# A layer norm moved from ScalarE to VectorE inside a matmul-bound decoder layer, with its loads asked for one job sooner

## The chip, the cores and the metric

The kernel runs on one core of one Trainium2 chip. The metric is the device time of one execution in microseconds (us), and the median of several executions stands for a kernel. A profile of one more execution gives the start and duration of every instruction on each engine: TensorE (PE; its weight loads are listed as PEld), VectorE (DVE), ScalarE (ACT), GpSimd (POOL) and SyncE (SP), which here issues nearly all DMAs.

## The reference

One layer of a hybrid decoder is computed for 64 sample tokens and 1024 prompt tokens, in float32. Only the branch that the change touches is shown in full:

```python
h = rmsnorm(x, norm_mix)
q, k, v, gu, gv, ga, gb = split_in(h @ w_in)
o = sink_attention(q, k, v, mask, sinks)               # window 128, banded blocks
vn = layernorm(gelu(gv), ln_g, ln_b)                   # over 768 channels, one row per token
s = gelu(gu) * (tril(W_s[g]) @ vn + b[g])              # inside 128-token chunks, 6 groups
x = x + (sigmoid(ga) * (o @ w_pa) + sigmoid(gb) * (s @ w_pb)) @ w_out
x = x + conv_ffn(rmsnorm(x, norm_ffn))                 # up, causal conv of width 3, gelu gate, down
y = rmsnorm(x, norm_final)
```

`vn` of the sample tokens is also an output (`gvs`), beside keys, values and convolution states.

## The kernel before

Every large product is made of three passes of a rounded type: an operand is split into a high part (an ACT cast) and a low part (a DVE subtraction, line 41), and TensorE adds high times high, high times low and low times high. Nearly all of TensorE's time goes into such matmuls. Weights are streamed from HBM by SP, summed (line 178) and split on ACT and DVE a few units ahead of their use.

The tokens form two groups: group 0 has 576 columns (the 64 samples and four blocks of 128 prompt tokens), group 1 has 512 (four blocks). The work begins with the token-major projections `gv` and `v` (line 535). For these, `stats_tok` (line 495) sums the squares of each token on TensorE with one-column matmuls against ones, and ACT and DVE turn the sums into a scale that every evacuation of that stage uses. The result of `gelu(gv)` is written to HBM, one tensor `gvd` of 128 by 768 for each block of tokens.

Then come 19 pairs of output blocks by a seven-product scheme (class `Chain`, line 317): the loop over `seq` runs seven products j for each pair, twelve matmuls for each group in each product. A chain writes its products into a few PSUM banks again and again, and between two products on one bank ACT copies the intermediate sum out (`keep`, lines 296 and 298) or DVE adds it to a result (`put`, line 303). After the last product ACT writes one quarter (line 343), and `a_finish` applies gelu (line 852) or sigmoid (line 854) on ACT.

Side work is handed out between the products from lists of small jobs. After the ninth pair the list `lns` gives one job after each of the products 0, 2, 4 and 6: nine layer-norm jobs (`ln_job`), six entries that prepare the mixing and its samples, and twelve `mix_job`s that multiply the normalised blocks with the lower-triangular weights (lines 788 and 816, results in a PSUM tile called `mx`). What is left in the list is run at once when the last three pairs begin, and after it the list `prep` prepares the attention of the samples; there POOL copies the sample queries into a padded tile (line 892).

A layer-norm job loads one block `v` into one of two buffers, normalises it with one ACT instruction (line 759), multiplies by the gain and adds the bias on DVE (lines 761 and 762), and stores it to `vnd`, from which the mixing jobs read. The first job also opens the pool of these tiles, loads gain and bias, and computes mean, deviation and the factors `sd` and `mr` (lines 735 to 738); four of the jobs load half blocks of group 1 through the staging ring of four buffers and take their statistics (lines 754 and 755).

The program text does not fix the order on the engines alone. A planner sorts the instructions of each engine by their place in the text, its own cost estimates and the moment when buffers come free, so that an instruction that is ready can be issued ahead of earlier ones; a tile of a pool waits until an earlier tile in its buffer has been read for the last time. `keep_in_program_order` marks instructions that the planner may not move in this way.

The kernel ends with the down projection (line 1686) and the final norm. For the last 256 columns `fin_rms` sums squares by one-column matmuls (line 1719), ACT and DVE form the scale, and `fin_rb` spreads it over the partitions by matmuls with the identity (line 1731). Three matmuls of constants (line 1857) stand in the text between the two.

Of the kernel before, what the change touches and what calls it, by code (L numbers as in the profile page):

```python
# [6 lines left out]
F32 = mybir.dt.float32  # L7
F32R = mybir.dt.float32r
I32 = mybir.dt.int32
AF = mybir.ActivationFunctionType  # L10
ALU = mybir.AluOpType
# [4 lines left out]
P = 128  # L16
# [9 lines left out]
GW = 768  # L26
# [8 lines left out]
def layer(tc, a):  # L35
    nc = tc.nc
    V, S, G, PE = nc.vector, nc.scalar, nc.gpsimd, nc.tensor
# [11 lines left out]
    with ExitStack() as top:  # L49
# [18 lines left out]
        ones = cst.tile([P, P], F32, name="c_ones")  # L68
# [276 lines left out]
        def pick(x, place, lo, hi):  # L345
# [3 lines left out]
        groups = [dict(g=0, n=576, off=0, soff=NS, base=192, mbase=448, blk0=0,  # L349
                       chunks=[(192, 0, 320), (512, 320, 576)],  # L350
                       toks=[("s", 0), *((i, NS + P * i) for i in range(4))]),
                  dict(g=1, n=512, off=576, soff=0, base=0, mbase=0, blk0=4,
                       chunks=[(0, 0, 512)], toks=[(4 + i, P * i) for i in range(4)])]
# [15 lines left out]
        gvd = {name: dr(f"gvd{name}", [P, GW]) for gr in groups for name, _ in gr["toks"]}  # L369
# [13 lines left out]
        with ExitStack() as ph1:  # L383
# [9 lines left out]
            def stage(n):  # L393
                return stg.tile([P, 576], F32, name="stg")[:, :n]

            late = {}
# [90 lines left out]
            lnst = c1.tile([P, 9, 3, 6], F32, name="lnst")  # L487
            line(c1, 96)
            pso = ExitStack()
            psa = pso.enter_context(tc.tile_pool(name="psa", bufs=7, space=PSUM))  # L490

            def bank():
                return psa.tile([P, 512], F32, name="st")

            def stats_tok(g):

                acc = rsg[g]
                pt = bank()[:, :len(groups[g]["toks"])]
                for i, (_, lo) in enumerate(groups[g]["toks"]):
                    PE.matmul(pt[:, i:i + 1], acc[:, lo:lo + P], ones[:, 0:1], start=True, stop=True)  # L500
                S.activation(rstg[g], pt, AF.Sqrt, bias=eps, scale=1.0 / D)  # L501
                V.reciprocal(rstg[g], rstg[g])
# [120 lines left out]
            def first_out():  # L623
                stats_tok(0)
                for i in range(len(toks0)):
                    gv_out(0, i, 0, ps5[i])
# [58 lines left out]
            none = lambda: None  # L685
            jobs = [lambda: x_in(0)] + [x for kk in range(4) for x in (t0_job(kk), none)] + [t1_job(kk) for kk in range(4)]
            tokens(1, ("v", 1), lambda i, ps: v_out(1, i, ps), jobs, lambda: stats_tok(1))
            stats_all(1)
            wide["again"] = True
# [8 lines left out]
            def poola(name, bufs, stack=None, **kw):  # L698
                return (stack or pa).enter_context(tc.tile_pool(name=name, bufs=bufs, reuse_waits="tile", **kw))
# [27 lines left out]
            lno = ExitStack()  # L727

            def ln_scale(g):

                n = len(groups[g]["toks"])
                mv = late["lnp"].tile([P, 5, 2], F32, name="mv", bufs=2)[:, 0:n]
                sd, mr = (late[x][:, 5 * g:5 * g + n] for x in ("sd", "mr"))
                for t in range(n):
                    V.bn_aggr(mv[:, t], lnst[:, 5 * g + t, 0:3 - g])
                S.activation(sd, mv[:, :, 1], AF.Sqrt, bias=eps)
                V.reciprocal(sd, sd)
                V.scalar_tensor_tensor(mr, mv[:, :, 0], -1.0, sd, ALU.mult, ALU.mult)

            def ln_job(g, i):  # L740
                def go():
                    if "lnp" not in late:
                        lnp = late["lnp"] = poola("ln", 1, lno)
                        for x in ("lng", "lnb"):
                            late[x] = lnp.tile([P, GW], F32, name=x)
                            nc.sync.dma_start(late[x], a[x])
                        for x in ("sd", "mr"):
                            late[x] = lnp.tile([P, 9], F32, name=x)
                    if i == 0:
                        ln_scale(g)  # L750
                    if g == 0 and i < 4:
                        for e in range(2):
                            x = stage(384)
                            nc.sync.dma_start(x, gvd[groups[1]["toks"][i][0]][:, 384 * e:384 * e + 384])
                            V.bn_stats(lnst[:, 5 + i, e], x)
                    lnp, name = late["lnp"], groups[g]["toks"][i][0]
                    v = lnp.tile([P, GW], F32, name="v", bufs=2)
                    nc.sync.dma_start(v, gvd[name])
                    S.activation(v, v, AF.Identity, bias=late["mr"][:, 5 * g + i:5 * g + i + 1],
                                 scale=late["sd"][:, 5 * g + i:5 * g + i + 1])  # L760
                    V.tensor_mul(v, v, late["lng"])  # L761
                    V.tensor_add(v, v, late["lnb"])
                    nc.sync.dma_start(vnd[g][:, :, i], v.rearrange("p (g c) -> p g c", c=P))
                    if name == "s":
                        nc.sync.dma_start(a["gvs"], v[0:NS])
                return go

            lns = [ln_job(gr["g"], i) for gr in groups for i in range(len(gr["toks"]))]

            def mix_first():  # L770
                lno.close()
# [889 lines left out]
        with ExitStack() as ph3:  # L1661
# [64 lines left out]
            def fin_rb(ps, rt, nb, m):  # L1726

                both = [ps, psl.tile([P, 512], F32, name="fs", bufs=2)]
                for p in both:
                    for i in range(nb):  # L1730
                        PE.matmul(p[:, i * m:i * m + m], rt[:, i:i + 1].to_broadcast([m, P]), ident[0:m, 0:m],
                                  start=True, stop=True)
                return [p[:, :nb * m] for p in both]
# [20 lines left out]
            def fin_copy(th, e, rb):  # L1754
                rs = lp.tile([P, 288], F32, name="rb", bufs=2)[:, :spans[e][1] - spans[e][0]]
                copy = S.copy(rs, rb[-1])
                if not (th and e):
                    tc.keep_in_program_order(copy)
                return rb[0], rs
# [16 lines left out]
            bank = [psd.tile([P, 512], F32, name="dn") for _ in range(6)]  # L1776
# [77 lines left out]
                y_out(1, 0, c, c + 4)  # L1854
            fin[3] = fin_rms(1, 1, last)
            for _ in range(3):
                PE.matmul(bank[0][:, 0:P], ones, ones, start=True, stop=True)
            rb, rs = fin_copy(1, 1, fin_rb(*fin[3]))
            for c in range(0, KD, 2):
                fin_mul(1, 1, *((rb, (c,), V) if c < 6 else (rs, (c,), G)))  # L1860
# [94 lines left out]
```

## Time and profile before

| What | Value |
|---|---|
| median of 3 runs | 1507.31 us (1506.05 to 1512.88) |
| the profiled execution | 1507.61 us |
| its span on the core | 1505.9 us |
| mean granted TensorE clock | 0.998 |
| TensorE matmul busy | 1491.5 us (99%) |
| TensorE weight loads busy | 1451.8 us (96%) |
| VectorE busy | 1176.4 us (78%) |
| ScalarE busy | 856.3 us (57%) |
| GpSimd busy | 265.7 us (18%) |

The profile's times count from the start of the span; the profiled execution is 1.7 us longer than its span. A timeline row gives start, duration, engine, line and operation, the tile written and the tiles read, and how often it was repeated; in square brackets stands how long the engine had been idle before it, and what it waited for. Neighbouring instructions of one form are merged in a row. A row of windows gives for each engine its busy time and in brackets the instructions that started there, then the granted clock, the busy share of the DMA engines and what they moved in GB/s.

### The profile page before, as it was taken

How to read it: one execution, taken by the hardware profiler on the slowest of the kernel's cores; microseconds unless marked ns; L12 is line 12 of the kernel's file. 1: busy time of each engine (PE TensorE's matmuls, PEld its weight loads, DVE VectorE, ACT ScalarE, POOL GpSimd, SP SyncE). 2: the span in 40 equal slices, each digit the busy share in tenths (PEclk: the TensorE clock that was granted, in tenths of full speed). 3: DMA queues.
4: the chain of work that ended last, by engine and by line, in shares of the span. 5: the costliest groups of instructions: out<-in, count | busy, mean ns of one | idle time of the engine just before them, and what ended most of it. 6: DMA issues, size and time to landing. Idle time of an engine off the chain costs nothing.

```text
span 1505.9 us, 30082 instructions
## 1 busy us (share of the span) xinstructions
PE 1491.5 (99%) x11508; PEld 1451.8 (96%) x11508; DVE 1176.4 (78%) x1886; ACT 856.3 (57%) x1790; POOL 265.7 (18%) x375
## 2 busy tenths in 40 slices
PE   9999999999999999999999999999999999999998
PEld 9999999999998989998989999999999999999998
DVE  7798776755576887989667988898899888785586
ACT  7657676654465765864443555555555556363464
POOL 0001000110030222320134321332242222000002
PEclk9999999999999999999999999999999999999999
DMA  7688446864779757438988423232242226993453
GB/s 253 225 275 274 155 163 224 243 207 150 239 243 294 219 180 231 162 123 308 335 295 287 141 109 122 98 142 108 83 151 109 84 83 223 326 303 98 113 172 148
DMA packets 134431, 289.88 MB, mean 192 GB/s; under 512 B 15760, under 2 KB 36560, under 8 KB 134288
## 3 DMA queue, kind: packets, MB, share of 16 engines
q1 hardware_dynamic: 134144, 287.96, 56.8%
q8 instruction: 90, 1.47, 0.4%
q14 instruction: 53, 0.43, 0.1%
q10 hardware_dynamic: 144, 0.01, 0.0%
HBM read 198.97 MB, written 90.92 MB: 192 GB/s over the span
## 4 chain that ended last, share of the span: by engine, by line
PE 85%; DVE 5%; ACT 4%; DMA 3%; issue 2%; POOL 1%; SPq 0%; POOLq 0%; ACTq 0%; DVEq 0%
PE st L317 45%; PE dn L1686 14%; PE mm L242 13%; PE st L535 6%; PE po L1233 2%; PE sc L1182 1%; DVE wl L41 1%; PE pt L1209 1%; DMA v<-gvd 1%; PE mx L816 1%; ACT wh L41 1%; ACT s L1199 1%; DMA kd<-q 0%; DMA v<-gvds 0%; DVE v L761 0%
## 5 line engine op out<-in xcount | busy, mean ns | idle before, releaser
L317 PE MATMUL st<-t,wh 128*128 128x288 f32 x2128 | 428.6, 295 | 3.4 <-ACT k L296 2.3
L317 PEld LDWEIGHTS st<-t,wh 128*128 128x128 f32 x2128 | 335.7, 188 | 4.6 <-ACT k L296 3.0
L317 PE MATMUL st<-t,wl 128*128 128x288 f32 x1064 | 312.2, 293 | 0.0
L317 PE MATMUL st<-th,wh 128*128 128x256 f32 x1064 | 296.0, 278 | 0.6 <-ACT k L296 0.5
L317 PE MATMUL st<-tl,wh 128*128 128x256 f32 x1064 | 294.7, 277 | 0.0
L317 PE MATMUL st<-th,wl 128*128 128x256 f32 x1064 | 294.5, 277 | 0.0
L317 PEld LDWEIGHTS st<-th,wh 128*128 128x128 f32 x1064 | 200.0, 188 | 1.9 <-ACT k L296 1.4
L317 PEld LDWEIGHTS st<-t,wl 128*128 128x128 f32 x1064 | 200.1, 188 | 0.0
L317 PEld LDWEIGHTS st<-th,wl 128*128 128x128 f32 x1064 | 199.8, 188 | 0.0
L317 PEld LDWEIGHTS st<-tl,wh 128*128 128x128 f32 x1064 | 199.8, 188 | 0.0
L1686 PE MATMUL dn<-th,wh 128*128 128x288 f32 (+1 forms) x616 | 177.1, 288 | 0.6 <-ACT zb L343 0.6
L1686 PE MATMUL dn<-tl,wh 128*128 128x288 f32 (+1 forms) x616 | 176.8, 287 | 0.0
L41 ACT CAST wh<-wraw 128x512 fp32r<-128x512 f32 (+2 forms) x188 | 129.4, 701 | 82.0 <-DMA wraw<-wt 30.1
L1686 PE MATMUL dn<-th,wl 128*128 128x288 f32 (+1 forms) x616 | 175.3, 285 | 0.0
L41 DVE TENSOR_TENSOR wl<-wraw,wh 128x512 fp32r<-128x512 f32 (+2 forms) x188 | 148.0, 800 | 28.5 <-ACT wh L41 26.2
L41 ACT CAST wh<-ws 128x512 fp32r<-128x512 f32 x168 | 102.5, 621 | 93.9 <-PE st L317 53.0
L41 DVE TENSOR_TENSOR wl<-ws,wh 128x512 fp32r<-128x512 f32 x168 | 117.5, 710 | 44.5 <-ACT wh L41 43.7
L1686 PEld LDWEIGHTS dn<-th,wh 128*128 128x128 f32 x616 | 115.7, 188 | 1.0 <-ACT zb L343 0.8
L1686 PEld LDWEIGHTS dn<-th,wl 128*128 128x128 f32 x616 | 116.1, 188 | 0.1
L1686 PEld LDWEIGHTS dn<-tl,wh 128*128 128x128 f32 x616 | 115.7, 188 | 0.1
L535 PE MATMUL st<-w2h,hh 128*128 128x256 f32 x288 | 80.6, 280 | 0.4 <-ACT rst L501 0.4
L535 PE MATMUL st<-w2h,hl 128*128 128x256 f32 x288 | 80.1, 279 | 0.1
(281 smaller groups left out, 3169.1 us busy)
## 6 DMA issues: line engine op xcount, KB each, us to landing
wraw<-wt SPq DMA_DIRECT2D x137, 512.0 KB
traw<-td SPq DMA_DIRECT2D x77, 272.0 KB
td<-za SPq DMA_DIRECT2D x22, 544.0 KB
q<-qd SPq DMA_DIRECT2D x16, 512.0 KB
upd<-hl SPq DMA_DIRECT2D x14, 512.0 KB
td<-t SPq DMA_DIRECT2D x11, 544.0 KB
wpart<-wt SPq DMA_DIRECT2D x22, 256.0 KB
qd<-q SPq DMA_DIRECT2D x8, 576.0 KB
```

The costliest lines, as they stand in the source:

```text
L41: for x in (S.copy(hi, src), V.tensor_sub(lo, src, hi.bitcast(F32))):
L242: PE.matmul(ps[:, lo:lo + c1 - c0], u[:, k, :], v[:, c0:c1], start=(k == 0 and i == 0), stop=(k == nk - 1 and i == 2))
L317: PE.matmul(ps, u[:, kk, :], v, start=first and kk + i == 0, stop=kk == 3 and i == 2, skip_group_check=True)
L535: PE.matmul(ps, u[:, lo:lo + P], v[:, k, :], start=k + i == 0, stop=k == KD - 1 and i == 2)
L816: PE.matmul(ps[:, P * i:P * i + P], vn[:, i], late["wst"][:, c, :], start=True, stop=True)
L1182: PE.matmul(ps[:, h, o0:256], q, kst[kv][:, e, k0:cur + P], start=e == 0, stop=e == 1)
L1199: S.activation(s[:, h], s[:, h], AF.Exp, bias=nm[:, h:h + 1], accum_out=dn[:, h:h + 1])
L1209: PE.transpose(pt[:, h * P:h * P + P], s[:, h, 0:P], ident)
L1233: PE.matmul(po, v[:, kv, :], t, start=e == 0, stop=last)
L1686: PE.matmul(place(m, e), u[:, m, :], v[:, lo:hi], start=new and i + k == 0 and (e == 0 or m % 2 == 0), stop=i == NU - 1 and k == 2, skip_g ...
```

## The change

Three places are edited.

In `stats_tok` the small PSUM tile comes from the one-bank tag `mx` and no longer from the seven banks called `st`.

In the layer norm the ACT instruction is gone. Two DVE instructions with two operations each do the whole normalisation: (v + mr) * gain, then (result * sd) + bias; for this `mr` is now minus the mean and no longer minus the mean times the scale. The loads of a job are moved into a function `ln_load`, which the job before calls at its end. A new first entry of the list opens the pool and asks for the tiles of job 0, so the list is one entry longer, and every job in it comes one place later than before; each load of a block keeps the place that its job had.

At the end the three constant matmuls are marked to stay in program order.

```diff
             def stats_tok(g):
 
                 acc = rsg[g]
-                pt = bank()[:, :len(groups[g]["toks"])]
+                pt = psa.tile([P, 512], F32, name="mx", bufs=1)[:, :len(groups[g]["toks"])]
...
                 S.activation(sd, mv[:, :, 1], AF.Sqrt, bias=eps)
                 V.reciprocal(sd, sd)
-                V.scalar_tensor_tensor(mr, mv[:, :, 0], -1.0, sd, ALU.mult, ALU.mult)
-
-            def ln_job(g, i):
+                V.tensor_scalar(mr, mv[:, :, 0], -1.0, None, ALU.mult)
+
+            ln_toks = [(gr["g"], i, name) for gr in groups for i, (name, _) in enumerate(gr["toks"])]
+            ln_in = {}
+
+            def ln_load(at):
+
+                if at == 0:
+                    lnp = late["lnp"] = poola("ln", 1, lno)
+                    for x in ("lng", "lnb"):
+                        late[x] = lnp.tile([P, GW], F32, name=x)
+                        nc.sync.dma_start(late[x], a[x])
+                    for x in ("sd", "mr"):
+                        late[x] = lnp.tile([P, 9], F32, name=x)
+                if at < len(ln_toks):
+                    g, i, name = ln_toks[at]
+                    xs = [stage(384) for e in range(2)] if g == 0 and i < 4 else []
+                    for e, x in enumerate(xs):
+                        nc.sync.dma_start(x, gvd[groups[1]["toks"][i][0]][:, 384 * e:384 * e + 384])
+                    v = late["lnp"].tile([P, GW], F32, name="v", bufs=2)
+                    nc.sync.dma_start(v, gvd[name])
+                    ln_in[at] = xs, v
+
+            def ln_job(at):
                 def go():
...
+                    g, i, name = ln_toks[at]
+                    xs, v = ln_in.pop(at)
                     if i == 0:
                         ln_scale(g)
...
-                    S.activation(v, v, AF.Identity, bias=late["mr"][:, 5 * g + i:5 * g + i + 1],
-                                 scale=late["sd"][:, 5 * g + i:5 * g + i + 1])
-                    V.tensor_mul(v, v, late["lng"])
-                    V.tensor_add(v, v, late["lnb"])
+                    for e, x in enumerate(xs):
+                        V.bn_stats(lnst[:, 5 + i, e], x)
+                    col = slice(5 * g + i, 5 * g + i + 1)
+                    V.scalar_tensor_tensor(v, v, late["mr"][:, col], late["lng"], ALU.add, ALU.mult)
+                    V.scalar_tensor_tensor(v, v, late["sd"][:, col], late["lnb"], ALU.mult, ALU.add)
                     nc.sync.dma_start(vnd[g][:, :, i], v.rearrange("p (g c) -> p g c", c=P))
                     if name == "s":
                         nc.sync.dma_start(a["gvs"], v[0:NS])
+                    ln_load(at + 1)
                 return go
 
-            lns = [ln_job(gr["g"], i) for gr in groups for i in range(len(gr["toks"]))]
+            lns = [lambda: ln_load(0)] + [ln_job(at) for at in range(len(ln_toks))]
...
             fin[3] = fin_rms(1, 1, last)
             for _ in range(3):
-                PE.matmul(bank[0][:, 0:P], ones, ones, start=True, stop=True)
+                tc.keep_in_program_order(PE.matmul(bank[0][:, 0:P], ones, ones, start=True, stop=True))
```

More of the change, by code (lines that the diff above doesn't have):

```diff
@@ L737, in ln_scale @@
                 V.reciprocal(sd, sd)
-                V.scalar_tensor_tensor(mr, mv[:, :, 0], -1.0, sd, ALU.mult, ALU.mult)
-            def ln_job(g, i):
-                def go():
[L742 to L748, printed above, removed]
+                V.tensor_scalar(mr, mv[:, :, 0], -1.0, None, ALU.mult)
@@ L749, in go @@
+            def ln_job(at):
+                def go():
+                    g, i, name = ln_toks[at]
+                    xs, v = ln_in.pop(at)
                     if i == 0:
                         ln_scale(g)
[L751 to L759, printed above, removed]
-                                 scale=late["sd"][:, 5 * g + i:5 * g + i + 1])
-                    V.tensor_mul(v, v, late["lng"])
-                    V.tensor_add(v, v, late["lnb"])
+                    for e, x in enumerate(xs):
+                        V.bn_stats(lnst[:, 5 + i, e], x)
```

## The prediction

> **What bounds the kernel now.** I read the page's busy line first, then TensorE's own waits, then windows of 20 us to find where those waits lie, and last the timeline around each.
>
> ```profile
> span 1505.9 us, 30082 instructions
> PE 1491.5 (99%) x11508; PEld 1451.8 (96%) x11508; DVE 1176.4 (78%) x1886; ACT 856.3 (57%) x1790; POOL 265.7 (18%) x375
> ```
>
> TensorE is busy for 1491.5 of 1505.9 us. The change takes no matmul away, so all it can win lies in the missing 14.4 us and in matmuls that go slowly; what it can lose has no such limit. Less work on ACT, DVE or POOL counts only where TensorE waits for them. The profiled execution took 1507.61 us, 0.30 above the median of 1507.31, and 1.7 above its span; I sum against 1507.61 and take off 0.30 at the end.
>
> ```profile
> PE st L317 <- ACT k L296: 2.8, 4, 1.5
> PE st L317 <- ACT kn L298: 1.0, 1, 1.0
> ...
> 260.00:280.00 20.00, 20.00 (x166) 20.00 (x165) 12.70 (x18) 11.51 (x23) 2.57 (x2) 1.00 0.71 230
> 280.00:300.00 20.00, 19.14 (x153) 18.80 (x153) 15.41 (x21) 12.79 (x25) 2.73 (x2) 1.00 0.82 239
> 300.00:320.00 20.00, 17.50 (x141) 17.10 (x140) 13.49 (x19) 10.27 (x20) 2.31 (x2) 1.00 0.66 202
> ```
>
> TensorE's largest waits are for ACT's copies out of PSUM, and the windows put them into the layer norm: from 280 to 320 us TensorE is idle for 0.86 + 2.50 = 3.36 us. It starts 153 + 141 matmuls where the undisturbed window starts 166 each, 38 too few; at 20.00/166 = 0.120 us that is 4.6 us. So 3.4 (idle alone) to 4.6 (with slow matmuls after each stop) is what this stage can return.
>
> **The three stops.** The timeline shows each stop, and what stood ahead of the copy on ACT.
>
> ```profile
> 294.99 0.53 PE L317 MATMUL st<-t,wh 128*128 128x288 f32 x2 [0.86 <-ACT k L296]
> 308.19 0.53 PE L317 MATMUL st<-t,wh 128*128 128x288 f32 x2 [1.02 <-ACT kn L298]
> 318.78 0.54 PE L317 MATMUL st<-t,wh 128*128 128x288 f32 x2 [1.49 <-ACT k L296]
> ...
> 280.75 1.03 ACT L759 ACTIVATE v<-v,mr,sd 128x768 f32<-128x768 f32 x1 [3.54 <-DMA v<-gvd]
> 289.38 0.69 ACT L852 ACTIVATE z<-z 128x576 f32<-128x576 f32 x1 [3.11 <-DVE z L303]
> 291.75 1.02 ACT L759 ACTIVATE v<-v,mr,sd 128x768 f32<-128x768 f32 x1
> 294.55 0.39 ACT L296 COPY k<-st 128x288 f32<-128x288 f32 x1
> 303.69 1.03 ACT L759 ACTIVATE v<-v,mr,sd 128x768 f32<-128x768 f32 x1 [4.83 <-DMA v<-gvd]
> 305.77 1.03 ACT L759 ACTIVATE v<-v,mr,sd 128x768 f32<-128x768 f32 x1 [1.05 <-DVE v L761]
> 307.74 0.67 ACT L298 ACTIVATE kn<-st 128x288 f32<-128x288 f32 x2
> 315.85 1.03 ACT L759 ACTIVATE v<-v,mr,sd 128x768 f32<-128x768 f32 x1 [1.18 <-DMA v<-gvd]
> 318.35 0.38 ACT L296 COPY k<-st 128x288 f32<-128x288 f32 x1
> ...
> 281.81 0.96 DVE L761 TENSOR_TENSOR v<-v,lng 128x768 f32<-128x768 f32 x1 [3.06 <-ACT v L759]
> 288.91 0.44 DVE L303 TENSOR_TENSOR z<-k,st 128x288 f32<-128x288 f32 x1
> ```
>
> ACT runs in order. While its line-759 instruction waits for a load, the copies behind it wait too, and TensorE cannot write the bank again. With line 759 gone, even if no load lands sooner:
> - Second stop: ahead of the kn at 307.74 stood 4.83 us of waiting, two v of 1.03 and a wait of 1.05. Without the last three alone kn comes 3.1 us sooner, against 1.02 needed.
> - Third stop: 1.18 + 1.03 = 2.2 us sooner, against 1.49.
> - First stop: 1.02 us from the v at 291.75. ACT also waited 3.11 us for DVE's z of 288.91, which stood behind DVE's wait of 3.06; DVE starts at the landing, 280.75, rather than at 281.81, another 1.06. Together 2.1 against 0.86.
>
> **The layer norm, edit by edit.**
>
> ```profile
> L759 ACT ACTIVATE v<-v,mr,sd x9: 1020/1032/1035, 262.8 to 315.8; 128x768 f32<-128x768 f32 x9
> L761 DVE TENSOR_TENSOR v<-v,lng x9: 947/958/959, 263.9 to 316.9; 128x768 f32<-128x768 f32 x9
> L1426 DVE SCALAR_TENSOR_TENSOR x<-x,c_gains,sc 128x576 f32<-128x576 f32 x8 | 6.2, 804 | 0.0
> L1565 DVE SCALAR_TENSOR_TENSOR c<-za,cw,c 128x1104 f32<-128x1104 f32 x22 | 30.1, 1367 | 16.6 <-ACT c L1564 16.5
> ...
> SPq L758 <- DMA vnd<-v: 3.4, 3, 3.0
> ```
>
> ACT loses 9 x 1.03 = 9.3 us. DVE keeps 18 instructions. The new form is shown at 576 and 1104 elements (0.80 and 1.37 us); a straight line between them gives 1.01 us at 768, an estimate, against 0.958 for the old. That is 0 to 18 x 0.05 = 0.9 us more DVE work, hidden by DVE's idle time (15.41 and 13.49 busy of 20 in the two windows); without that cover it would cost the 0.9. `mr` stays two instructions on a handful of columns, with one input fewer, and counts nothing.
>
> The DMAs are the same in number and size. Each load keeps its place in the text and its job comes one place later, which gives the load a place more to land in. I count nothing for that: there are two buffers, and SP three times waited at a load for the store that frees one (3.4 us, up to 3.0). The half-block loads and their statistics have other buffers and nobody near. Behind each load on SP stand weight loads and stores; that queue is as long as before.
>
> So the stage returns 3.4 to 4.6 us by the static shift. DVE can now stop at a late load itself, with the weight splits and the puts behind it. I take 3.4, the idle time.
>
> **The list.** Eighteen entries behind the nine jobs move by one place, 48 matmuls or 5.8 us. They fill the seven pairs exactly (28 places), so no batch is left over. TensorE does the same matmuls elsewhere. What follows, the samples' preparation, I count as zero between a loss of 5.8 and nothing; no row excludes a gain but none suggests one.
>
> **The end.**
>
> ```profile
> 1496.33 0.71 ACT L1705 ACTIVATE sq<-x 128x256 f32<-128x256 f32 x2
> 1496.83 0.75 PEld L1857 LDWEIGHTS dn<-c_ones 128*128 128x128 f32 x6
> 1497.50 0.97 PEld L1719 LDWEIGHTS fs<-c_ones,sq 128*128 128x128 f32 x8
> 1498.60 0.26 ACT L1722 ACTIVATE rt<-fs,c_eps 128x2 f32<-128x2 f32 x1 [0.76 <-PE fs L1719]
> 1499.11 1.16 PE L1731 MATMUL fs<-c_ident,rt 128*128 128x128 f32 x8 [0.55 <-DVE rt L1723]
> ```
>
> The planner put the constant matmuls (six, as each is two passes) ahead of the last eight sums, from 1496.83 to 1497.50. The last squares end at 1497.04. In text order four sums can start at 1496.83 and four at about 1497.3, and all behind comes 0.67 us sooner. The constants then take 0.67 us of the 1497.50 to 1499.11 in which TensorE now works 0.97 us and waits 0.55; they end about when line 1731 becomes ready, which may give back 0.1. I take 0.6, between 0 (the mark does not move them) and 0.67. All that follows hangs on line 1731, so it reaches the end.
>
> **The statistics' bank.**
>
> ```profile
> 24.76 0.38 PE L535 MATMUL st<-w2h,hh 128*128 128x256 f32 x1 [0.36 <-ACT rst L501]
> 25.66 1.28 ACT L566 ACT_TABLE_LOAD   x1
> 26.95 1.21 ACT L566 ACTIVATE gv<-st,rst 128x256 f32<-128x256 f32 x3
> ```
>
> The 0.36 us goes, since the next tile finds a free bank. But that tile is 24 matmuls of about 0.12 us (the rate of the windows), 2.8 us, and the one after it needs a bank that the first of the three gv frees at 26.95 + 1.21/3 = 27.35. Today it begins at about 24.76 + 2.8 = 27.5; it cannot begin before 27.35. What is late next is this gelu, behind its table load of 1.28 us. Between 0 and 0.36, I take 0.1, near the gv row.
>
> **Sum.** 3.4 + 0.6 + 0.1 = 4.1; 1507.61 - 4.1 = 1503.5, on the median's scale 1503.2.
>
> **The rivals.**
> - Full return: 4.6 + 0.67 + 0.36 = 5.6, to 1501.7. For it: each stop's margin is 0.7 us or more. Against it: the planner orders anew.
> - The wait changes its engine: DVE stops at the loads, and half of the stage's gain stays away. 1507.31 - 1.7 - 0.6 = 1505.0. For it: ACT waited up to 4.83 us for a load, and DVE has more queued behind it. Against it: DVE stood through 3.06 us already, behind ACT. It holds if loads land no sooner, and with two buffers a load waits for the store two jobs before it. In the Trainium skill, "DMA: Bandwidth & Descriptors", section "Anatomy of one DMA — SWDGE (gpsimd) path", a transfer costs about 2.0 us fixed plus its bytes over 436 GB/s, an estimated 2.9 us for these 384 KB and 5.8 us for a store and the load behind it. By that rule a buffer is away for a whole place, asking sooner wins nothing, and DVE goes on waiting, so the result would be this rival's 1505.0. The trace, with ACT's waits of 3.54 and 4.83 us for loads, agrees so far; it is why the case has 0.2.
> - Slower, by the later places: the samples' queries are copied on POOL just ahead of the chains' POOL work.
>
> ```profile
> 428.36 6.97 POOL L892 COPY qs<-stg 64x64 f32<-64x64 f32 x16
> 435.73 0.91 POOL L327 TENSOR_TENSOR kn<-kn,ku 128x256 f32<-128x256 f32 x1 [0.40 <-ACT ku L296]
> ```
>
> Only 0.40 us lies between. If the copies move by the full place, 5.8 us, POOL's kn comes up to 5.4 us late, then z, the sigmoid on ACT that waits for z, and the next copies out of PSUM. It decides where more than 4.1 of these reach TensorE; the whole gives 1503.2 + 5.4 = 1508.6. Against it: the copies need only their load, and today start late because of their tile.
> - The mark moves nothing: 1503.8.
>
> **How the numbers follow.** My forecast (1502.4 to 1504.4, with the unmoved mark) has 0.45, the full return 0.17, DVE's wait 0.2, the slower rival 0.1; 0.08 is left for an order that the planner changes far from here, either way. The likeliest is 1503.2. The range 1501.0 to 1508.7 takes in all four cases. A measurement of this kernel can tell about 0.5%, 7.5 us, from no change: no case named reaches that. Faster by more needs 1499.8, beyond the full return, 0.05; slower by more needs 1514.8, 0.04; within, 0.91.
>
> **What would show it.** Right: no line-759 row, TensorE near 20.00 in both windows from 280 to 320 with about 166 matmuls each; line 1857 behind the last line 1719, and 1722 some 0.6 us nearer to the last line 1686; no wait for rst but one for gv within 0.5 us near 27. DVE's wait would read as DVE v waiting for the DMA, with TensorE waiting for wl or z there. The slower rival would show as line 327 behind the copies and idle TensorE from 435 to 450. Wrong I would be if new stops appear in stages that the text leaves alone.

## The result, and the profile after

The changed kernel takes 1514.9 us (median; 1509.6 to 1519.9) where the kernel before takes 1507.6 us: a ratio of 1.0045, 95% interval 1.0034 to 1.0056. It is slower, by less than 0.5% but outside the range predicted. The profiled execution took 1513.9 us.

Busy times of the kernel after, from the page:

```profile
span 1512.2 us, 30063 instructions
PE 1493.4 (99%) x11508; PEld 1453.4 (96%) x11508; DVE 1174.3 (78%) x1886; ACT 849.2 (56%) x1781; POOL 273.2 (18%) x375
```

ACT lost 7.1 us and DVE 2.1 us of work; POOL, which the change does not touch, is busy 7.5 us longer with the same 375 instructions. That row is the first hint. TensorE's waits in the kernel after (engine, line, released by: us in total, times, longest):

```profile
PE st L317 <- ACT k L296: 3.8, 4, 1.9
PE dn L1696 <- DVE x L1706: 2.9, 2, 2.0
PE pt L1133 <- DVE s L1126: 1.4, 1, 1.4
...
PE sc L1099 <- issue: 0.8, 1, 0.8
```

Waits for `x` of line 1706, `pt` of 1133 (1.4, before 0.4) and an unexplained pause at `sc` are new. To place them I took the start of the same TensorE matmul in both traces and subtracted. Columns are times in the trace of before; each row is one execution, up to 2.8 us away from the median of its kernel; the kernels below the first two rows come from the experiments.

```
TensorE later than before (us), at   28.1  285.5    346   452   490  1290  1312  1495
after                                -0.6   -0.9   -3.7  -1.5   0.7   1.5   6.4   6.2
after_again                           0.5    0.0   -3.5   0.7   1.4   1.3   5.0   5.2
four_more_on_act                     -0.3   -0.4   -3.0   1.1   1.1   1.0   1.0   0.9
state_on_act                         -0.1    0.7   -2.1   2.3   3.3   7.9   7.9   7.7
copies_late                          -0.3    1.9   -0.7   0.3   3.1   3.1   3.1   3.3
shift_alone                          -0.0    1.2    0.9   3.0   6.7   7.4   7.4   7.3
one_empty_less                        0.1    1.4   -1.7  -1.7  -1.3  -0.2  -0.2  -0.4
two_ops_alone                        -0.4    0.4   -0.9  -0.4  -0.2  -0.4  -0.4  -0.5
mark_alone                            0.1    0.7   -0.4  -0.1   0.6   0.7   0.7   0.6
bank_alone                            0.1    0.4    0.2   0.2   1.0   2.4   2.4   2.2
three_buffers                        -0.0   -0.6   -4.1  -4.1  -3.8  -3.5  -3.5  -3.6
three_old_bank                       -0.4   -0.4   -4.3  -4.2  -2.7  -2.5  -2.5  -1.9
```

Read the first row by differences: the layer norm won 2.8 us (285 to 346), then 4.4 us were lost between 346 and 490, and 4.9 us between 1290 and 1312. The other rows say how far such a difference can be trusted. With the old layer norm mark_alone still wins 1.1 us from 285 to 346, bank_alone loses 1.4 us once between 490 and 1290, and the two executions of after differ by 2.0 us from 346 to 452.

**The layer norm.** Windows of the kernel after (us, then busy time and count of PE, PEld, DVE, ACT, POOL, clock, DMA share, GB/s):

```profile
280.00:300.00 20.00, 20.00 (x164) 19.95 (x163) 15.04 (x23) 8.90 (x20) 3.85 (x2) 1.00 0.79 250
300.00:320.00 20.00, 18.84 (x154) 18.64 (x153) 15.54 (x24) 9.94 (x22) 1.50 (x2) 1.00 0.67 217
```

153 and 141 matmuls have become 164 and 154. Two of the three stops are gone; the third is left, and ahead of it DVE now waits for a load and does the layer norm, while ACT waits for DVE:

```profile
315.10 0.54 PE L317 MATMUL st<-t,wh 128*128 128x288 f32 x2 [1.16 <-ACT k L296]
...
305.23 1.02 DVE L770 SCALAR_TENSOR_TENSOR v<-v,mr,lng 128x768 f32<-128x768 f32 x1 [1.42 <-DMA v<-gvd]
...
310.44 0.69 ACT L862 ACTIVATE z<-z 128x576 f32<-128x576 f32 x1 [6.69 <-DVE z L303]
```

**After the mixing.** Timeline of the kernel after:

```profile
420.97 0.32 SPq L831 DMA_DIRECT2D sd<-stg  x1
...
425.52 0.58 SPq L897 DMA_DIRECT2D stg<-qsd  x1
...
428.94 8.16 POOL L902 COPY qs<-stg 64x64 f32<-64x64 f32 x16 [5.11 <-DMA stg<-qsd]
437.18 0.74 POOL L327 TENSOR_TENSOR kn<-kn,ku 128x256 f32<-128x256 f32 x1
437.99 1.06 POOL L303 TENSOR_TENSOR z<-kn,k 128x256 f32<-128x256 f32 x1
...
439.09 1.15 ACT L864 ACTIVATE z<-z 128x512 f32<-128x512 f32 x2 [2.77 <-POOL z L303]
440.71 0.36 ACT L296 COPY k<-st 128x256 f32<-128x256 f32 x1
...
441.12 0.39 PE L317 MATMUL st<-th,wh 128*128 128x256 f32 x1 [1.88 <-ACT k L296]
```

and the one row of before that the prediction did not show:

```profile
419.06 0.42 SPq L887 DMA_DIRECT2D stg<-qsd  x1
```

TensorE is 3.7 us ahead here, and yet the queries' load is issued 6.5 us later than before: the planner put it behind the store of the next to last mixing job (line 831) and the stores of z, because the mixing jobs now end one place later. POOL waits 5.11 us for it, kn comes 1.5 us later than before on the clock (435.73), 5.2 us against TensorE, then z, the sigmoid, the copy out of PSUM, TensorE.

What this stop costs depends on the clock. In after the clock stays at 1.00 behind it, and 2.2 us go from 346 to 452. In the second execution, after_again, the stop is 2.40 us long, the granted clock behind it is 0.50, and 4.2 us go:

```profile
443.00:445.00 2.00, 2.00 (x12) 2.00 (x11) 2.00 (x5) 1.51 (x4) 0.00 (x0) 0.50 0.90 287
```

**At 1300 us.** First the kernel before, ACT, POOL and SP:

```profile
1252.79 1.31 ACT L1564 ACTIVATE c<-za,cw 128x1104 f32<-128x1104 f32 x1 [2.15 <-DVE za L303]
...
1259.87 0.28 POOL L1577 COPY za<-stc 128x18 f32<-128x18 f32 x1 [4.31 <-DMA za<-zd]
1262.96 1.26 POOL L1562 COPY stc<-za 128x2 f32<-128x2 f32 x1 [0.98 <-DVE za L303]
...
1265.53 0.34 SPq L1812 DMA_DIRECT2D tails<-stc  x1
```

then the kernel after, in which every engine has the same order of instructions here:

```profile
1254.38 1.31 ACT L1574 ACTIVATE c<-za,cw 128x1104 f32<-128x1104 f32 x1 [2.43 <-DVE za L303]
...
1261.16 3.03 POOL L1587 COPY za<-stc 128x18 f32<-128x18 f32 x1 [4.01 <-DMA za<-zd]
1266.00 4.43 POOL L1572 COPY stc<-za 128x2 f32<-128x2 f32 x1
...
1262.77 1.36 DVE L41 TENSOR_TENSOR tl<-traw,th 128x544 fp32r<-128x544 f32 x2
1264.04 0.42 DVE L303 TENSOR_TENSOR za<-ku,st 128x256 f32<-128x256 f32 x1
...
1270.29 1.38 DVE L1575 SCALAR_TENSOR_TENSOR c<-za,cw,c 128x1104 f32<-128x1104 f32 x1
...
1272.54 0.34 SPq L1822 DMA_DIRECT2D tails<-stc  x1
...
1301.15 0.69 DVE L467 TENSOR_TENSOR s<-wraw 128x512 f32<-128x512 f32 x1 [2.69 <-DMA wraw<-wt]
...
1302.35 0.37 PE L1696 MATMUL dn<-th,wh 128*128 128x288 f32 x1 [2.02 <-DVE x L1706]
```

and a window of it:

```profile
1304.00:1306.00 2.00, 2.00 (x9) 2.00 (x10) 2.00 (x5) 1.30 (x3) 0.00 (x0) 0.50 1.06 414
```

POOL's copies of a few columns take 3.03 and 4.43 us; the store of the tails waits for the last of them at the head of SP's queue and goes out 7.0 us later (TensorE is 1.4 us later there); the weight loads behind it are late, DVE waits for one, then takes `x` late, and TensorE stops. In the window TensorE works at half the granted clock behind the stop, 9 matmuls in 2 us, so that 2.9 us of waits cost 4.9.

### The profile page after: what moved, and what is told of

Same layout as the page of the kernel before. It is cut to its first block, busy times and chain, and to the rows that moved or that the text cites. A ratio compares the mean times of both kernels' runs of the same rounds, so it can differ in the third digit from the quotient of the medians.

```text
span 1512.2 us, 30063 instructions
## 1 busy us (share of the span) xinstructions
PE 1493.4 (99%) x11508; PEld 1453.4 (96%) x11508; DVE 1174.3 (78%) x1886; ACT 849.2 (56%) x1781; POOL 273.2 (18%) x375
## 4 chain that ended last, share of the span: by engine, by line
PE 86%; DVE 5%; DMA 3%; ACT 3%; POOL 2%; issue 2%; SPq 0%; POOLq 0%; DVEq 0%; ACTq 0%
PE st L317 48%; PE mm L242 13%; PE dn L1696 12%; PE st L535 6%; PE po L1243 2%; PE sc L1192 1%; DMA stg<-sd 1%; PE pt L1219 1%; DMA wl<-upd 1%; DVE wl L41 1%; PE mx L826 1%; DMA wraw<-wt 1%; ACT s L1209 1%; ACT wh L41 0%; DMA za<-zd 0%
## 5 line engine op out<-in xcount | busy, mean ns | idle before, releaser
L535 PE MATMUL st<-w2l,hh 128*128 128x256 f32 x288 | 79.9, 278 | 0.0
```

Source lines behind the costliest of these rows:

```text
L535: PE.matmul(ps, u[:, lo:lo + P], v[:, k, :], start=k + i == 0, stop=k == KD - 1 and i == 2)
```

## The experiments

**The list's places.** Edits: an empty entry ahead of the old list (kernel before); one empty entry less (kernel after).

```
-            lns = [ln_job(gr["g"], i) for gr in groups ...
+            lns = [none] + [ln_job(gr["g"], i) for gr in groups ...
```
```
-            lns += [mix_first, none, none, mix_samples, ...
+            lns += [mix_first, none, mix_samples, ...
```

> The kernel before with one empty entry put ahead of its list of jobs, nothing else: the layer norm and the mixing come one place later, with the old three-instruction layer norm. Theory (the later places cost the time between 440 and 475 us): the queries' load is issued after the mixing stores, POOL's copies end about 5 us later against TensorE than before, TensorE stops near 444 us, and TensorE is 3.5 to 4.5 us later than before at 475 us: 1507.6 + 4 = 1511.6 us. Rival (the places cost nothing; the loss comes from the new layer norm or the marked matmuls): TensorE at 475 us within 1 us of before, 1507.6 us.

> The kernel after with one of the two empty entries behind mix_first removed, so that the list has 27 entries again and the samples' mixing and all mixing jobs have the places of before, while the layer norm keeps its own. Theory (later places): the queries' load is issued ahead of the last mixing store again, no stop at 439 us, TensorE keeps the 3.7 to 4.0 us won in the layer norm past 475 us; 1514.9 - 4.4 = 1510.5 us. Rival (places cost nothing): 1514.9 us with the stops between 439 and 480 us unchanged.

Measured: shift_alone 1512.8 us, ratio to before 1.0033 (1.0017 to 1.0049); one_empty_less 1506.5 us, 0.9995 (0.9983 to 1.0007). In shift_alone the load goes out at 430.09 us and POOL's kn comes at 441.24 instead of 435.73, with TensorE 0.9 us late there, so 4.6 us later against it:

```profile
434.00 7.16 POOL L892 COPY qs<-stg 64x64 f32<-64x64 f32 x16 [5.59 <-DMA stg<-qsd]
441.24 1.14 POOL L327 TENSOR_TENSOR kn<-kn,ku 128x256 f32<-128x256 f32 x1
```

From 346 to 490 us TensorE loses 3.8 to 5.8 us in all kernels with the later places (after, four_more_on_act, state_on_act, copies_late, shift_alone) and 0.3 to 1.6 us in the six without. The theory holds: the list costs it, whatever the layer norm is made of. one_empty_less is left with one stop in the layer norm and with DVE's waits for loads:

```profile
PE st L317 <- ACT k L296: 1.6, 3, 1.1
...
DVE v L770 <- DMA v<-gvd: 11.6, 4, 6.0
```

That it came out 4 us better than I expected is because nothing is lost at 1300 us, to which the runs after the next turn.

**POOL's copies of the queries.** Edit: the queries go into a cache tile, and the copies stand, in program order, behind the first chain's kn and z.

```
-                    f = stage(KD * NS)...
+                    f = sp.tile([P, 8, P], F32, name="cache", bufs=3)...
...
                         load_s(0, c + 2)
+                        if c == 0:
+                            copies()
```

> The kernel after, all its later places kept, but the queries are loaded into a slot of the cache tiles, and the 16 copies on POOL stand in program order behind the first chain's kn and z instead of ahead of them. Theory (POOL's copies, waiting for the late load, hold up kn, z, the sigmoid and the copies out of PSUM): the stop of 2.2 us at 439 us goes, and TensorE at 475 us is 2.2 to 4.4 us sooner than in the kernel after: 1510.5 to 1512.7 us. Rival (the staging tiles or the other later jobs, not POOL's copies): the stop at 439 us stays, 1514.9 us.

Measured: 1508.2 us, 1.0004 (0.9992 to 1.0016). POOL's kn is at its place against TensorE again (435.02, with TensorE 0.7 us ahead; 435.73 in before), and only 1.0 us is lost from 346 to 452 us, where the kernel after lost 2.2 and 4.2. But 2.8 us more go from there to 490, most of it in one wait. The timeline's row and the wait's:

```profile
435.02 0.90 POOL L327 TENSOR_TENSOR kn<-kn,ku 128x256 f32<-128x256 f32 x1 [8.21 <-ACT ku L296]
```
```profile
PE pt L1140 <- DVE s L1133: 2.1, 1, 2.1
```

So the copies made the stop at 439 us, as the theory says, but taking them away only moved most of the loss to the first softmax: from 346 to 490 us 3.8 us go, against 4.4 and 4.9 in the two executions of after, and TensorE is not the 2.2 to 4.4 us sooner that the theory expected. Which of the later jobs does the rest I did not separate. The time is better than the theory's because nothing is lost at 1300 us (the traced execution, 1511.1 us, is 2.8 us above the median); that needs the next runs.

**POOL's small copies.** Edit: `S.copy` for `G.tensor_copy` in `conv` and `put_state`; and the kernel after a second time.

> The kernel after, but the small copies of the convolution's state (stc and the first columns of za and zb, 0.2 us each on an idle POOL, up to 4.43 us in the profile of after) run on ACT. Theory (POOL's small copies were held up by DVE's stream of two-input operations, the store of the tails waited for them on SP, and the weight loads behind it came 7 us late): the store of the tails is issued within 3 us of the last copy, no stop at 1307 us, 1514.9 - 4.8 = 1510.1 us, and the runs lie closer together than the 10 us of after. Rival (the weight loads come late for another reason): the stop near 1307 us stays and the time is 1514.9 us or, with more work on ACT, above it.

> The kernel after itself, a second time. Theory (the 4.8 us lost near 1307 us in its profile is a matter of timing: in the same order of instructions POOL's small copies took 9 us in that execution and 5 in others): this profile may or may not show it; the store of the tails is issued either 5.4 to 6 us after POOL's first copy (no loss, about 1510 us) or over 9 us after it (1513 to 1520 us), and where it is late TensorE stops near 1307 us. Rival (the loss is fixed by the change): the stop of 2.9 us or more for DVE's line 1706 is there again, near 1307 us.

Measured: state_on_act 1515.6 us, 1.0048 (1.0031 to 1.0065); after_again 1514.2 us, 1.0047 (1.0029 to 1.0065). In state_on_act the stop at 1300 us is gone (7.9 at 1290 and at 1312), as expected, but ACT now waits for DVE and for loads ahead of a copy that TensorE needs, and 5.0 us go between 1100 and 1290 us, most of them near 1110:

```profile
1113.59 0.19 ACT L1572 COPY stc<-za 128x2 f32<-128x2 f32 x1 [2.49 <-DVE za L303]
1115.12 0.21 ACT L1587 COPY zb<-stc 128x18 f32<-128x18 f32 x1 [1.33 <-DMA zb<-zd]
```

after_again decides against my theory of chance: the same copies take 2.80 and 4.43 us, to within 0.25 us of the first time. The loss belongs to this kernel.

```profile
1261.07 2.80 POOL L1587 COPY za<-stc 128x18 f32<-128x18 f32 x1 [4.23 <-DMA za<-zd]
1265.69 4.43 POOL L1572 COPY stc<-za 128x2 f32<-128x2 f32 x1
```

What differs first is ACT's activation of line 1574. In both executions of after ACT is idle 2.43 us ahead of it, in the others with this order 2.15 or 2.16, behind the same DVE instruction; in the trace's records the difference lies between the end of its semaphore wait and its start (0.32 against 0.05 us). From there DVE runs 0.28 us later. Its waits for ACT then end before the instruction ahead of them begins, in before while that runs; that this is what leaves POOL no slot I argue, and have not shown.

**The place in ACT's stream.** Edit: four one-column copies, kept in program order, some 400 us earlier; the order of all other instructions stays the same on every engine.

```
         nc.sync.dma_start(stc, a["stc"])
+        for _ in range(4):
+            tc.keep_in_program_order(S.copy(warm, eps))
```

> The kernel after with four one-column copies added to ScalarE's program at the start of the second phase (some 400 us ahead of the stop at 1307 us); every other instruction of every engine keeps its order. In both profiles of after, ACT's activation of line 1574 starts 0.34 us behind the wait ahead of it at 1252.7 us of before's time, in the others 0.06 us, and from there DVE runs 0.28 us later. Theory (this pause of 0.28 us belongs to a place in ACT's instruction stream; without it DVE's stream leaves POOL its slots, and the whole loss near 1307 us goes): with four more instructions the pause falls on another instruction, POOL's copies take under 1.3 us each, the store of the tails is issued within 6 us of the first copy, no stop at 1307 us, 1514.9 - 4.5 = 1510.4 us. Rival (the pause or the loss belongs to the data or the order, not to the place in the stream): the stop is there again and the time is 1514.9 to 1515.7 us.

Measured: 1510.35 us, 1.0013 (1.0002 to 1.0025), against 1510.4 expected. Four more instructions made the kernel 4.6 us faster:

```profile
1253.77 1.31 ACT L1574 ACTIVATE c<-za,cw 128x1104 f32<-128x1104 f32 x1 [2.16 <-DVE za L303]
...
1263.94 1.26 POOL L1572 COPY stc<-za 128x2 f32<-128x2 f32 x1 [0.97 <-DVE za L303]
...
1266.53 0.34 SPq L1824 DMA_DIRECT2D tails<-stc  x1
```

ACT's idle time is 2.16 us again: the pause is gone, and with it the whole chain. TensorE is 1.0 us late at 1250 us here as in after_again, and the order of the other instructions is the same, so what is left to decide on the pause is what stands ahead in ACT's stream. Such a pause, 0.32 us from the end of a wait to the start, stands at a few other places too: at 1447 us in four_more_on_act, at 446 and 1150 us in both kernels with three buffers. That it goes with the place in the stream fits this, and is not proved. What makes it at such a place is not shown, and the nine missing layer-norm instructions alone do not: two_ops_alone lacks them too and has no pause here.

**The other parts one by one.** Edits: on the kernel before, only the two VectorE operations with `mr` (loads and list as they were); only the mark; only the bank.

> The kernel before with the two new VectorE operations in place of ScalarE's and the two old ones; loads, list and everything else as before. Theory (the gain of the layer norm is ACT's line 759 out of the way, not the sooner loads): TensorE's three stops near 295, 308 and 319 us shrink to at most one, 2.5 to 4 us won between 280 and 345 us, kept to the end: 1507.6 - 3.2 = 1504.4 us. Rival (without the sooner loads DVE waits for them and the stops move to DVE's weight splits): under 1.7 us won, 1506 us or more.

> The kernel before with the last three constant matmuls kept in program order, nothing else. Theory: the reciprocal behind the last sums ends 0.6 us sooner after the first of these sums (2.7 us against 3.3 us before), and the end comes 0.6 us sooner where the granted clock stays at 1.00 until the identity matmuls, 1507.6 - 0.6 = 1507.0 us; where the clock falls to 0.50 before them, they take 1.9 instead of 1.2 us and nothing is won. Rival (the mark changes the planner's order far from the end, and part of the loss is its): over 1509 us.

> The kernel before with the statistics in the bank mx, nothing else. Theory: TensorE's wait of 0.36 us for the statistics near 24.8 us is gone, and 0.1 to 0.36 us of it is still there at 28 us, after the wait for the gelu that comes next; no other stage changes: 1507.3 us. Rival (the mx bank, allocated earlier, changes the planner's order or the banks of the chains): TensorE's offset against before moves by more than 1 us somewhere later.

two_ops_alone: 1509.3 us, 1.0012 (1.0001 to 1.0024). TensorE wins 1.3 us from 285 to 346, hardly more than mark_alone (1.1) with the old layer norm. One stop of 2.9 us is left, and DVE waits for the loads:

```profile
PE st L317 <- ACT k L296: 4.1, 5, 2.9
...
DVE v L760 <- DMA v<-gvd: 14.1, 5, 6.5
```

The theory is wrong and the rival right: without the sooner loads the wait goes from ACT to DVE. The traced execution, 1507.1 us, is 2.2 us below the median, so what made the others slower is not in this trace.

mark_alone: 1507.9 us, 1.0002 (0.9992 to 1.0013). The constants move behind the sums and line 1731 becomes ready sooner; but see the end below. bank_alone: 1509.9 us in a single execution, in which 1.4 us go between 490 and 820 us that no other kernel lost. The wait of 0.36 us is gone, one of 0.25 for the gelu follows, and at 459 us a new pause stands ahead of the scores:

```profile
459.34 1.09 PE L1089 MATMUL sc<-cache,qs 128*64 128x128 f32 x16 [0.87 <-issue]
```

**What is left of the layer norm's stop.** Edits on one_empty_less: three buffers for `v`; then also the old bank.

```
-                    v = late["lnp"].tile([P, GW], F32, name="v", bufs=2)
+                    v = late["lnp"].tile([P, GW], F32, name="v", bufs=3)
```

> The kernel one_empty_less (the kernel after with one empty entry less) with three instead of two buffers for the layer norm's v. Theory (the stop that is left in the layer norm comes from DVE waiting for loads that wait for the store of the job before last): DVE's waits for v, 12.8 us in one_empty_less, fall to under 6 us, TensorE's last stop of 1.1 us near 315 us goes, and the time is 1 us less: 1505.5 us. Rival (the loads wait on SP behind weight loads and stores, not for their buffer): DVE waits as long, 1506.5 us.

> The kernel three_buffers with the statistics back in the bank of before. In every profile with the statistics in mx TensorE pauses 0.81 to 0.88 us ahead of the first matmul of the samples' scores near 459 us, for nothing that the profile names; in none of before, shift_alone, mark_alone and two_ops_alone. In these kernels that matmul waits for POOL as well. Theory (the bank brings the pause, which is more than the wait of 0.36 us that it saves): the pause is gone, the wait for the statistics near 24.8 us is back, and the time is 0.5 to 0.8 us less than three_buffers: 1505.2 - 0.6 = 1504.6 us. Rival (the pause has another cause): it stays, and the time is 1505.2 to 1505.6 us.

three_buffers: 1505.2 us, 0.998 (0.9965 to 0.9995). Faster than the kernels before and after; against one_empty_less (0.9983 to 1.0007) the times alone do not settle it. Its windows, and DVE's remaining wait for `v` (11.6 us in one_empty_less; less, but not under 6):

```profile
280.00:300.00 20.00, 19.84 (x162) 19.63 (x162) 16.69 (x24) 9.10 (x21) 4.16 (x2) 1.00 0.82 267
300.00:320.00 20.00, 19.90 (x163) 19.70 (x162) 13.30 (x20) 9.86 (x22) 3.83 (x3) 1.00 0.68 219
```
```profile
DVE v L770 <- DMA v<-gvd: 8.0, 2, 4.3
```

three_old_bank: 1505.4 us, 0.9981 (0.997 to 0.9991), the same. The pause ahead of the scores is gone, but TensorE then waits 1.6 us for the first softmax:

```profile
PE pt L1133 <- DVE s L1126: 1.6, 1, 1.6
```

So the pause belongs to the bank (in seven kernels with it, in none of five without). It costs nothing in three_buffers, since what comes next is late anyway: from 455 to 490 us 0.6 us go with it and 1.3 us without. In bank_alone 0.9 us go there that the kernel before does not lose.

## Why the prediction was wrong

- **The list** is the step that failed. I counted its later places as zero "between a loss of 5.8 and nothing". They cost 3.8 to 5.8 us. The rival with a chance of 0.1 had the place and the price right (kn up to 5.4 us late; 5.2 us in after, 4.6 in shift_alone) and the first link of the mechanism; copies_late shows that POOL's copies are only a part, since 3.8 us go without their stop. What I held against it, that the copies need only their load, is why it was true: the load moved too, 10 us against TensorE in both kernels, behind the mixing jobs' stores on SP. I had asked what POOL would do with a later copy, not where SP's order would put the load. This step alone takes the time out of the range: four_more_on_act, which loses nothing at 1300 us, takes 1510.35 us, and one_empty_less, without either loss, 1506.5.
- **Nothing stood in the sum for a stage that the change does not touch.** The other 3.7 to 4.9 us come from 1300 us, where no instruction moved. The prediction named "new stops in stages that the text leaves alone" as what would make it wrong, with no price; its 0.08 was for an order that the planner changes, and here no order changed. That 0.04 stood for 1514.8 us or more was a number without a cause. No row of before shows that ACT would pause 0.28 us there; but its rows did show the thin place: POOL's copies of a few columns taking 0.3 to 1.3 us among DVE's stream, and a store that waits for them ahead of weight loads on SP.
- **The layer norm** returned 2.8 us (2.6 to 3.5 with two buffers and the sooner loads), where 3.4 to 4.6 were predicted: somewhat too much in size, wrong in reason. The shift off ACT alone, which I took to clear all three stops "even if no load lands sooner", wins 1.3 us in two_ops_alone; the stop that is left hangs on DVE. The sooner loads, counted as nothing, bring the rest as far as single traces tell, and a third buffer clears the last stop. I had cited the Trainium skill's "DMA: Bandwidth & Descriptors", section "Anatomy of one DMA — SWDGE (gpsimd) path", for the case that asking sooner wins nothing. That section is about DMAs issued by GpSimd, and these loads are issued by SP. The traces agree that DVE goes on waiting (14.1 us without the sooner loads, 11.6 with them) and not that nothing is won: TensorE's longest stop fell from 2.9 to 1.1 us.
- **The rival of DVE's wait** is what two_ops_alone shows: 14.1 us of DVE's waits for loads. Its price, 1505.0 us, is not what that kernel takes (1509.3).
- **The end** brought nothing instead of 0.6. The matmuls did move, and line 1731 starts 0.5 to 0.6 us sooner after the first sum in six of the nine traces with the mark; in the other three (after_again, one_empty_less, three_buffers) the clock falls to 0.50 before it and it starts no sooner. But "all that follows hangs on line 1731, so it reaches the end" is wrong: the stores of y fill the DMA engines. From the kernel before and from four_more_on_act, whose clock also stayed at 1.00 until TensorE's last matmuls:

```profile
1498.90:1500.90 2.00, 1.16 (x8) 0.97 (x8) 1.20 (x3) 0.37 (x1) 0.09 (x1) 1.00 1.00 408
1500.90:1502.90 2.00, 0.00 (x0) 0.00 (x0) 0.84 (x2) 0.00 (x0) 1.18 (x1) 0.60 0.99 385
```
```profile
1499.80:1501.80 2.00, 0.65 (x6) 0.46 (x5) 1.75 (x3) 0.37 (x1) 0.81 (x1) 1.00 1.01 410
1501.80:1503.80 2.00, 0.00 (x0) 0.00 (x0) 0.13 (x1) 0.00 (x0) 0.46 (x1) 1.00 0.99 382
```

  TensorE and DVE are done earlier in the second, the DMA share is 1.0 in both, and from the first sum (1495.60 and 1496.46) to the end of the span it is 10.3 us in both.
- **The bank** is right at 28 us: no gain beyond what runs differ by, and the gelu is late next, 0.25 us. The pause at the scores, 0.9 us in bank_alone, was not foreseen.

## What to carry to other kernels

A list of jobs is part of the schedule: an entry more moves everything behind it, so follow the moved loads through the order of their queue before counting them as free. A gain at the end counts only if the DMA engines are not full there. And where small POOL copies stand between a dense DVE stream and a store at the head of the load queue, a quarter of a microsecond elsewhere cost five here; such a place should be priced as a risk of any change.

## What the runs showed of the hardware

- POOL's copies of 0.2 us take up to 4.43 us among DVE's instructions with two SBUF inputs. In the kernel after, the first of them ends when DVE comes to an instruction with an input in PSUM (POOL's copy ends at 1264.19, DVE's line 303 starts at 1264.04). The longest ends at 1270.43, as line 1575 starts, which has no input in PSUM; why it got in there is open. The Trainium skill, "SBUF — State Buffer", section "SBUF: two separate sides", says that a DVE instruction with two SBUF inputs and a GpSimd instruction that reads SBUF exclude each other for a whole instruction. The trace agrees, and adds that POOL can be passed over several times in a row: during its first copy four DVE instructions of line 41 begin, from 1261.57 to 1263.41.
- TensorE's granted clock falls to 0.50 behind some stops of about 2 us: from 1304 to 1306 us in after, and not behind the like stop in after_again; behind the stop at 440 us in after_again (2.40 us), and not in after (1.88 us), nor behind the longest stop, 2.89 us in two_ops_alone. The last identity matmuls take 1.1 us at 1.00 (four_more_on_act) and 1.8 to 1.9 at 0.50 (mark_alone, after). In the Trainium skill, "TensorE: Matmul & The Clock Gate", section "Part 1: The HAM clock gate (the "warmup" mystery)", the window that decides is free-running; that would make it differ from run to run, as here.
- Two pauses that the profile gives no reason for: 0.28 us more than elsewhere on ACT at one place of its stream (two of two executions of after, gone with four more instructions), and 0.81 to 0.88 us on TensorE ahead of the first scores, in the kernels with the statistics in `mx`, where that matmul waits for POOL as well.
